# Mixer B of an encoder layer: the per-token factor reaches all partitions through DRAM instead of through TensorE

## The chip, the core and the metric

The kernel runs on one core of one Trainium2 chip. The time is the device time of one execution in microseconds (us), the median of three runs. Profiles are of one execution each. PE is TensorE's matmul, PEld its weight load, DVE is VectorE, ACT ScalarE, POOL GpSimd; SP is the engine that issues all DMAs here.

## The reference, cut to what matters

One encoder layer is applied to two batches that share weights: "p" with 512 tokens and "s" with 1024. A normalised input is projected to 9728 columns, cut into the queries, keys, values and gates of three mixers and three merge gates. The three mixers' outputs, each times SiLU of its gate path, are projected, merged, projected again and added to the input. The change is in mixer B, differential attention:

```
a = jax.nn.softmax(s - slopes * dist, axis=-1)
w = a[:, :, 0] - lam * a[:, :, 1]
o = jnp.einsum('bhqk,bkhe->bqhe', w, v)
o = rms_norm(o, g_diff) * (1.0 - lam_init)
...
pb = (yb * jax.nn.silu(zb)) @ w_br_b
```

So each token and head has one number, its RMS factor together with the softmax denominator, that multiplies the 128 values of that token and head.

## The kernel before

**A program that is ordered by a planner.** The code records operations on tiles; `Program.order` then plays them through a list schedule with assumed prices (`price`, `shared`) and fixes one order for each engine, and `emit` (line 486, so every row of the profile carries L486) writes the instructions out in that order. An operation is placed when its operands are ready in the plan, its engine is free, a buffer slot of its class is free (`SLOTS`, `CAPS`), and it lies within `AHEAD` operations of the oldest one not placed. `copy` and `tt` record several ways (ACT or DVE, DVE or POOL), of which the planner picks one. On the chip every engine works through its own list strictly in order, SP too: a DMA whose operand is not ready holds all DMAs behind it.

**The stages.** First the projection of batch p (tiles `raw`, split into high and low parts `wh`, `wl`, `wb`, multiplied with `tp`/`th`/`tl` into PSUM tiles `p`, added up in `c`, stored to `Up`, `Us`, `Vp`, `Vs` in DRAM). From some 440 us on, the mixers of p, and then those of s, are interleaved with the projection of batch s: both give PE, DVE and ACT work at the same time. After some 1500 us come the branch projections and merge gates (`merge`) and the output projection (`output`).

**Mixer B** (`mixer_b`) has four units, one for each head, for each batch. A unit fetches its gate `z_tile` into `y`, makes scores `s`, exponentials `e` (or `tab`), transposes the weights (`t` to `pt`, `pl`) and multiplies with V into `o`, four blocks of 128 tokens into one PSUM bank `o`, with the value channels on partitions and 512 tokens along the free axis. After each 512 tokens it closes: squares of `o` are summed over the channels by four one-column matmuls with `ones`, so the sums stand with tokens on partitions, in a [128, 4] tile `r`, part of `czb`. DVE, POOL (a power of -1/2) and DVE make the factor there. It is needed along the free axis on all 128 partitions. Before the change, four `pe.transpose` of a broadcast column of `r` against `ident` put it into a PSUM tile `t`, and DVE multiplies `y` (gate times `o` times the gain `gd`) by that. `y` then goes to `YG` in DRAM, and is read again only in the merge stage. This closing runs 12 times: 4 units with one block of 512 tokens in p, 4 with two in s.

Mixer C (`mixer_c`) has the same need and already goes through DRAM: a transposed factor is written to `FD`, and read back with a partition step of zero into tiles `bb`. `bb` has two tiles of 2 KB per partition, of the class `k2` of 18 slots, which `ws`, `wh`, `wl`, `c`, `y`, `ft`, `pt` and others share.

Of the kernel before, what the change touches and what calls it, by code (L numbers as in the profile page):

```python
# [8 lines left out]
F32 = mybir.dt.float32  # L9
# [3 lines left out]
OP = mybir.AluOpType  # L13
# [50 lines left out]
def rows(a, off, dims):  # L64
    return bass.AP(tensor=a.tensor, offset=a.offset + off, ap=[list(d) for d in dims])
# [464 lines left out]
def build(ctx, tc, a):  # L530
    nc = tc.nc
    pg = Program(tc, nc, SLOTS, CAPS)
    act, dve, pool, pe = pg.act, pg.dve, pg.pool, pg.pe

    dma = pg.sync.dma_start

    def static(shape, name):
        return pg.tile("static", shape, F32, name)

    def load(dst, src, off, dims):  # L540
        dma(dst, src.rows(off, dims) if isinstance(src, View) else rows(src, off, dims))
# [18 lines left out]
    def tt(dst, x, y, op, engines="DP"):  # L560
        pg.any(*[({"D": dve, "P": pool}[e], "tensor_tensor", (dst, x, y), {"op": op}) for e in engines])

    def split(hi, lo, x, scale=None, psum=False):

        copy(hi, x, scale)
        if scale is None:
            tt(lo, x, hi.bitcast(F32), OP.subtract, "D" if psum else "DP")
        else:
            dve.scalar_tensor_tensor(lo, x, scale, hi.bitcast(F32), op0=OP.mult, op1=OP.subtract)

    ident = static([128, 128], "ident")
# [416 lines left out]
    def fetch(s, col, L):  # L988

        if L == 512:  # L990
            t = pg.tile("stp", [128, 512], F32)
            dma(t, U[s][col // 128][0])
        else:
            t = pg.tile("stg", [128, 1024], F32)
            dma(t.rearrange("p (b t) -> p b t", b=2), U[s][col // 128].rearrange("b p t -> p b t"))
        return t
# [29 lines left out]
    def q_tiles(x, L, view, scale=None):  # L1026
        q = qk_tiles(2, L)
        for f, g in pieces(x, view, L):
            for j in range(2):
                s, d = 64 * j, 64 - 64 * j  # L1030
                split(g(q[j], s, s + 64), g(q[j], d, d + 64), f(x, s, s + 64), scale)
        return q

    def k_tiles(x, L, view):
        kh, kl = qk_tiles(2, L), qk_tiles(2, L)
        for j in range(2):
            s, d = 64 * j, 64 - 64 * j
            pool.memset(kl[j][d:d + 64].bitcast(F32), 0.0)
            for f, g in pieces(x, view, L):
                split(g(kh[j], s, s + 64), g(kl[j], s, s + 64), f(x, s, s + 64))  # L1040
                copy(g(kh[j], d, d + 64), f(x, s, s + 64))
        return kh, kl
# [15 lines left out]
    def z_tile(s, col, b):  # L1058

        y = pg.tile("y", [128, 512], F32)  # L1060
        dma(y, U[s][col // 128][b])
        t = pg.tile("ft", [128, 512], F32)
        act.activation(t, y, AF.Tanh, scale=0.5)
        dve.scalar_tensor_tensor(y, t, 1.0, y, op0=OP.add, op1=OP.mult)
        return y

    def e_tile():
        return pg.tile("e", [128, 1024], F32)
# [99 lines left out]
    def mixer_b(sq, u, L):  # L1168
        nh = L // 512
        c0 = 128 * u  # L1170
        if sq not in dist:
            dist[sq] = pg.tile("tab", [128, 2304], F32)[:, :1920]
            dma(dist[sq], a["c_dist"])
        q = q_tiles(fetch(sq, QB + c0, L), L, nat, 0.125 / SLOPE_B[u])
        kh, kl = k_tiles(fetch(sq, KB + c0, L), L, nat)
        v = pg.tile("vp" if nh == 1 else "v", [128, 2, 4 * nh, 128], F32R)
        v = [v[:, 0], v[:, 1]]
        vr = pg.tile("stp" if nh == 1 else "stg", [128, 4 * nh, 128], F32)
        load(vr, V[sq][VB + 256 * (u // 2)], 128 * (u % 2), [[256, 128], [128 * 256, 4 * nh], [1, 128]])
        split(v[0], v[1], vr)  # L1180
        ww = []
        yield
        for i in range(L // 128):
            if nh == 1:
                pair = e_tile()
                pair = [pair[:, :512], pair[:, 512:]]
            elif i % 2:
                pair = pg.tile("tab", [128, 2, 1024], F32)
                pair = [pair[:, 0], pair[:, 1]]
            else:  # L1190
                pair = [e_tile(), e_tile()]
            if i % 4 == 0:
                y = z_tile(sq, ZB + c0, i // 4)
            st = small(6, "stb")
            es = []
            for hf in range(nh):
                pss = [pg.tile("s", [128, 512], F32) for _ in range(2)]
                qk_scores(pss, q, kh, kl, lambda t: t[:, 128 * i:128 * i + 128],
                          lambda t: t[:, 512 * hf:512 * hf + 512])
                x0 = 512 * hf - 128 * i + 896  # L1200
                for m in range(2):
                    dve.tensor_tensor_reduce(
                        out=pair[m][:, 512 * hf:512 * hf + 512], in0=pss[m], in1=dist[sq][:, x0:x0 + 512],
                        scale=-SLOPE_B[u], scalar=3e38 if hf == 0 else st[:, m:m + 1],
                        op0=OP.add, op1=OP.min, accum_out=st[:, 2 * hf + m:2 * hf + m + 1])
            for m in range(2):
                e = pair[m]
                nm = st[:, m:m + 1] if nh == 1 else st[:, 2 + m:3 + m]
                act.activation(e[:, :L], e[:, :L], AF.Exp, scale=-1.0, bias=nm, accum_out=st[:, 4 + m:5 + m])
                es.append(e)  # L1210
            if i % 4 == 0:
                cz = small(12, "czb")
            z0, c1 = cz[:, i % 4:i % 4 + 1], cz[:, 4:5]
            dve.reciprocal(z0, st[:, 4:5])
            dve.reciprocal(c1, st[:, 5:6])
            dve.scalar_tensor_tensor(c1, st[:, 4:5], c1, neglam, op0=OP.mult, op1=OP.mult)
            w = es[0][:, :L]
            dve.scalar_tensor_tensor(w, es[1][:, :L], c1, w, op0=OP.mult, op1=OP.add)
            ww.append(w)
            if i % 2 == 0:  # L1220
                yield
                continue
            if i % 4 == 1:
                o = pg.tile("o", [128, 512], F32)
            oq = o[:, 256 * (i // 2 % 2):256 * (i // 2 % 2) + 256]
            for b in range(2 * nh):
                ps = pg.tile("t", [128, 2, 256], F32)
                for k in range(2):
                    for j in range(2):
                        c = 256 * b + 128 * k  # L1230
                        pe.transpose(ps[:, k, 128 * j:128 * j + 128], ww[j][:, c:c + 128], ident)
                ph = pg.tile("pt", [128, 2, 256], F32R)
                pl = pg.tile("pl", [128, 2, 256], F32R)
                split(ph, pl, ps, psum=True)
                for k in range(2):
                    kb = 2 * b + k
                    for n, (x, z) in enumerate(((v[0], ph), (v[1], ph), (v[0], pl))):
                        pe.matmul(oq, x[:, kb], z[:, k], start=kb + n == 0, stop=kb == 4 * nh - 1 and n == 2)
            ww = []
            if i % 4 == 1:  # L1240
                yield
                continue
            sq_ = pg.tile("ft", [128, 512], F32)
            act.activation(sq_, o, AF.Square)
            ps = pg.tile("t", [128, 512], F32)
            for j in range(4):
                pe.matmul(ps[:, j:j + 1], sq_[:, 128 * j:128 * j + 128], ones, start=True, stop=True)
            r = cz[:, 8:12]
            dve.scalar_tensor_tensor(r, ps[:, :4], 1.0 / 128, cz[:, :4], op0=OP.mult, op1=OP.mult)
            dve.scalar_tensor_tensor(r, r, 1.0, cz[:, :4], op0=OP.mult, op1=OP.mult)  # L1250
            pool.tensor_scalar(r, r, EPS, None, op0=OP.add)
            pool.tensor_tensor(r, r, mhalf, op=OP.pow)
            dve.tensor_tensor(r, r, cz[:, :4], op=OP.mult)
            ps = pg.tile("t", [128, 512], F32)
            for j in range(4):
                pe.transpose(ps[:, 128 * j:128 * j + 128], r[:, j:j + 1].to_broadcast([128, 128]), ident)
            dve.scalar_tensor_tensor(y, o, gd, y, op0=OP.mult, op1=OP.mult)
            dve.tensor_tensor(y, ps, y, op=OP.mult)
            store_yg(sq, i // 4, 4 + u, y)
            yield  # L1260

# [392 lines left out]
    j = done = slot = 0  # L1654
    for i, k in slots("s", TS):
        slot = i + k / 7
        while j < len(units) and slot > starts[j]:
# [7 lines left out]
            j, done = j + 1, 0  # L1665
# [44 lines left out]
```

## Time and profile before

| what | value |
| --- | --- |
| median of three runs | 1846.41 us (1845.9 to 1847.65) |
| the profiled execution | 1845.54 us |
| its span, first to last instruction | 1843.8 us |
| PE / DVE / ACT / POOL busy | 98% / 84% / 66% / 18% of the span |
| mean granted TensorE clock | 0.996 |

The profiled execution took 1.74 us more than its span, and 0.87 us less than the median. In the rows below, a busy share is of the span or of the window that the row names; a row of groups gives the total busy time, the mean of one, and how long the engine stood idle right before such an instruction.

### The profile page before, as it was taken

The page shows a single profiled execution, that of the slowest core. Times are in us where ns is not written, and L with a number is a line of the kernel's source. Part 1 is how long each engine was busy: PE and PEld are TensorE (multiplying, and loading weights), DVE is VectorE, ACT ScalarE, POOL GpSimd, SP SyncE. Part 2 cuts the span into 40 slices and gives each one's busy share as a digit, 9 for nine tenths or more (in the row PEclk, how much of TensorE's full clock was granted, in tenths as well). Part 3 has the DMA queues.
Part 4 walks back from the last instruction along what each step waited for, and adds up shares of the span by engine and source line. Part 5 has one row for each costly group of instructions (what it writes and reads, how often), then busy time and mean ns, then how long its engine had stood idle before and what let it go on. Part 6 is the DMA issues. An engine that isn't in the chain of part 4 may idle for free.

```text
span 1843.8 us, 32386 instructions
## 1 busy us (share of the span) xinstructions
PE 1802.0 (98%) x11353; PEld 1466.4 (80%) x11448; DVE 1546.3 (84%) x3081; ACT 1209.4 (66%) x2411; POOL 328.1 (18%) x284
## 2 busy tenths in 40 slices
PE   7999999999999999999999999999999999999998
PEld 6999999999988777778787877776777776666776
DVE  8879999997887678788989898868779887876886
ACT  7677878894556766665656565777678786643343
POOL 0000000000000000000000000000001144987874
PEclk9999999999999999999999999999999999999999
DMA  7645545453424455642323231445455557977641
GB/s 245 184 145 178 172 149 193 152 182 115 140 90 142 135 151 158 183 149 92 103 84 127 65 120 69 132 125 168 133 150 158 179 162 257 325 235 252 213 150 69
DMA packets 242336, 287.14 MB, mean 156 GB/s; under 512 B 33182, under 2 KB 168574, under 8 KB 242174
## 3 DMA queue, kind: packets, MB, share of 16 engines
q1 hardware_dynamic: 242174, 285.08, 48.6%
q8 instruction: 90, 1.47, 0.3%
q14 instruction: 72, 0.59, 0.1%
HBM read 203.93 MB, written 81.44 MB: 155 GB/s over the span
## 4 chain that ended last, share of the span: by engine, by line
PE 93%; DVE 3%; ACT 2%; issue 1%; DMA 0%; SPq 0%; POOL 0%; DVEq 0%; POOLq 0%; ACTq 0%
PE p L486 64%; PE s L486 16%; PE o L486 6%; PE t L486 6%; ACT qk L486 1%; DVE qk L486 1%; DVE e L486 0%; ACT c L486 0%; DMA xp<-x_prompt 0%; DVE wl L486 0%; DVE c L486 0%; DVE tab L486 0%; DVE ws L486 0%; DVE xt L486 0%; ACT tab L486 0%
## 5 line engine op out<-in xcount | busy, mean ns | idle before, releaser
L486 PE MATMUL p<-th,wh 128*128 128x512 f32 x1400 | 428.5, 414 | 0.1
L486 PEld LDWEIGHTS p<-th,wh 128*128 128x128 f32 x1400 | 252.9, 189 | 53.7 <-issue 5.8
L486 PE MATMUL p<-th,wl 128*128 128x512 f32 x1016 | 295.2, 400 | 0.2 <-DVE wl L486 0.2
L486 ACT ACTIVATE wb<-raw 128x512 bf16<-128x512 f32 (+1 forms) x254 | 155.0, 614 | 145.0 <-PE p L486 89.8
L486 ACT ACTIVATE c<-p 128x512 f32<-128x512 f32 (+1 forms) x291 | 144.8, 498 | 125.4 <-PE p L486 122.3
L486 PEld LDWEIGHTS p<-th,wl 128*128 128x128 f32 x1016 | 186.3, 188 | 39.1 <-issue 2.9
L486 PEld LDWEIGHTS <-wb 128*128 128x128 bf16 x1392 | 109.1, 98 | 105.2 <-issue 50.2
L486 PE MATMUL s<-qk 128*128 128x512 f32 (+5 forms) x736 | 186.9, 361 | 4.7 <-DVE qk L486 2.2
L486 DVE TENSOR_TENSOR wl<-ws,wh 128x512 fp32r<-128x512 f32 x251 | 179.1, 716 | 11.8 <-ACT wh L486 6.5
L486 DVE CUSTOM_DVE_ANT_0 e<-s,tab 128x384 f32<-128x384 f32 (+3 forms) x256 | 130.3, 533 | 51.0 <-PE s L486 48.6
L486 DVE TENSOR_TENSOR c<-p,c 128x512 f32<-128x512 f32 (+1 forms) x219 | 125.2, 577 | 50.6 <-PE p L486 36.7
L486 ACT ACTIVATE pt<-t 128x512 fp32r<-128x512 f32 (+3 forms) x193 | 100.7, 539 | 101.3 <-PE t L486 99.1
L486 DVE TENSOR_TENSOR wl<-raw,wh 128x512 fp32r<-128x512 f32 x212 | 155.6, 746 | 6.1 <-ACT wh L486 2.6
L486 ACT ACTIVATE wh<-ws 128x512 fp32r<-128x512 f32 x240 | 147.7, 621 | 13.4 <-DVE ws L486 10.6
L486 ACT ACTIVATE wh<-raw 128x512 fp32r<-128x512 f32 (+1 forms) x228 | 136.7, 606 | 22.5 <-PE s L486 11.1
L486 PE MATMUL p<-tl,wb 128*128 128x512 bf16 x527 | 145.2, 381 | 5.3 <-issue 0.8
L486 PE MATMUL p<-tp,wh 128*128 128x256 f32 x888 | 147.2, 294 | 2.4 <-ACT wh L486 2.4
L486 PEld LDWEIGHTS s<-qk 128*128 128x128 f32 (+1 forms) x736 | 124.5, 189 | 29.3 <-issue 4.6
L486 PE MATMUL p<-tp,wl 128*128 128x256 f32 x888 | 142.7, 283 | 0.0
L486 ACT ACTIVATE e<-e,st 128x384 f32<-128x384 f32 (+2 forms) x192 | 105.2, 550 | 36.3 <-DVE st L486 35.4
L486 POOL MEMSET qk<- 64x512 f32 (+1 forms) x48 | 35.8, 747 | 515.8 <-PE t L486 171.1
L486 PE MATMUL p<-wq,th 128*128 128x256 f32 x816 | 124.6, 292 | 0.0
(231 smaller groups left out, 3752.7 us busy)
## 6 DMA issues: line engine op xcount, KB each, us to landing
raw<-w_in SPq DMA_DIRECT2D x140, 512.0 KB
Us<-c SPq DMA_DIRECT2D x128, 256.0 KB
Up<-c SPq DMA_DIRECT2D x64, 256.0 KB
stg<-Us SPq DMA_DIRECT2D x30, 512.0 KB
g<-Us SPq DMA_DIRECT2D x48, 256.0 KB
tab<-E SPq DMA_DIRECT2D x192, 48.0 KB
stp<-Up SPq DMA_DIRECT2D x30, 256.0 KB
YG<-y SPq DMA_DIRECT2D x30, 256.0 KB
```

The costliest lines, as they stand in the source:

```text
L486: getattr(engs[o.eng], o.meth)(*[val(x) for x in o.args], **{k: val(x) for k, x in o.kw.items()})
```

## The change

The four transposes and their PSUM tile go. The factor `r` ([128 tokens, 4 blocks]) is written to a DRAM tensor `RB` as four rows of 128 floats, which is 512 single floats side by side for the DMA, since neighbours in DRAM lie on different partitions. It is read back into a `bb` tile with a partition step of zero: 128 partitions get the same 512 floats. The multiplication of `y` takes `bb` in place of PSUM's `t`, and through `tt` the planner may give it to DVE or POOL.

```diff
--- before.py
+++ after.py
@@ -1251,11 +1251,12 @@
             pool.tensor_scalar(r, r, EPS, None, op0=OP.add)
             pool.tensor_tensor(r, r, mhalf, op=OP.pow)
             dve.tensor_tensor(r, r, cz[:, :4], op=OP.mult)
-            ps = pg.tile("t", [128, 512], F32)
-            for j in range(4):
-                pe.transpose(ps[:, 128 * j:128 * j + 128], r[:, j:j + 1].to_broadcast([128, 128]), ident)
+            RB = pg.tile("dram", [4, 128], F32, "RB")
+            dma(RB.rows(0, [[1, 128], [128, 4]]), r)
+            rb = pg.tile("bb", [128, 512], F32)
+            load(rb, RB, 0, [[0, 128], [1, 512]])
             dve.scalar_tensor_tensor(y, o, gd, y, op0=OP.mult, op1=OP.mult)
-            dve.tensor_tensor(y, ps, y, op=OP.mult)
+            tt(y, rb, y, OP.mult)
             store_yg(sq, i // 4, 4 + u, y)
             yield
```

The planner makes a new order, from the first closing on. All 12 multiplications stay on DVE. PE's order differs from row 2207 of 6238 to row 4467, which is from about 480 to some 1220 us; ahead of and behind that it is the same, and so are ACT's and DVE's; SP's order too is the same again from its row 446 of 744.

**PE, the first closing of batch p** (`czb` is the factor's tile, `wq`, `th` are projection operands, `ones`, `ft` the sums of squares):

```order
 L486 MATMUL s<-qk 128x512 x4
-L486 MATMUL p<-wq,th 128x256 x25
-L486 MATMUL t<-ident,czb 128x128 x4
-L486 MATMUL p<-wq,th 128x256 x23
+L486 MATMUL p<-wq,th 128x256 x48
 L486 MATMUL s<-qk 128x512 x4
 L486 MATMUL t<-ident,e 128x128 x2
```

The four transposes stood between 25 and 23 projection matmuls of one product; now the 48 stand in one piece.

**SP, the last closing of batch s in mixer B, before** (`v` is the V tile and `stg` a staging tile of the units that follow, `Us` a projection's result):

```order
L486 DMA v<-Vs_508 64x4x128 x2
L486 DMA YG_341<-y 128x512
L486 DMA stg<-Us_465 128x2x512
L486 DMA stg<-Us_453 128x2x512
L486 DMA Us_476<-c 128x512
```

and the same place in the changed kernel:

```order
L486 DMA v<-Vs_508 64x4x128 x2
L486 DMA RB<-czb 128x4x1
L486 DMA stg<-Us_465 128x2x512
L486 DMA bb<-RB 128x512
L486 DMA stg<-Us_453 128x2x512
L486 DMA YG_341<-y 128x512
L486 DMA Us_476<-c 128x512
```

The write and the read of `RB` are new in SP's list, a `stg` load stands between them, and the store of `y` has moved behind both `stg` loads.

**DVE, the same closing in the changed kernel**, from right behind the last step of the factor (`czb<-czb`) to its use:

```order
L486 CAST wh<-raw 128x512
L486 TENSOR_TENSOR wl<-raw,wh 128x512
L486 ISA e,st_15123<-s,tab 128x384
L486 ISA st_15123 128x1
L486 ISA e,st_15123<-s,tab 128x384
L486 ISA st_15123 128x1
L486 COPY pt<-t 128x384
L486 CAST wh<-ws 128x512
L486 TENSOR_TENSOR ws<-ws,raw 128x512
L486 TENSOR_TENSOR wl<-ws,wh 128x512
L486 TENSOR_TENSOR ws<-raw 128x512
L486 TENSOR_TENSOR y<-bb,y 128x512
```

The multiplication, the last row, has moved down: nine larger instructions now stand between the factor and its use.

## Rows read from the trace of the kernel before

**Rows 1.** the page's part 1: engine, busy us, share of the span, instructions

```profile
PE 1802.0 (98%) x11353; PEld 1466.4 (80%) x11448; DVE 1546.3 (84%) x3081; ACT 1209.4 (66%) x2411; POOL 328.1 (18%) x284
```

**Rows 2.** the page's part 4: shares of the chain that ended last, by engine

```profile
PE 93%; DVE 3%; ACT 2%; issue 1%; DMA 0%; SPq 0%; POOL 0%; DVEq 0%; POOLq 0%; ACTq 0%
```

**Rows 3.** busy time by stage: window, length, five engines, PEclk, DMA share, GB/s

```profile
480.00:1160.00 680.00, 675.91 (x3863) 538.15 (x3906) 578.93 (x1300) 425.90 (x813) 34.59 (x50) 1.00 0.38 119
...
1170.00:1180.00 10.00, 5.87 (x24) 3.59 (x22) 9.14 (x11) 9.93 (x12) 0.95 (x1) 0.85 0.59 228
1180.00:1190.00 10.00, 10.00 (x54) 8.78 (x53) 8.05 (x16) 5.74 (x8) 0.00 (x0) 0.81 0.42 131
...
1500.00:1843.80 343.80, 330.42 (x1534) 231.44 (x1560) 264.47 (x360) 170.37 (x354) 251.03 (x189) 0.99 0.64 213
```

**Rows 4.** groups by shape, PE: busy us, mean ns, idle before

```profile
L486 PE MATMUL t<-ident,czb 128*128 128x128 f32 x48 | 7.2, 272 | 0.0
```

**Rows 5.** chain of waits, two spots: start us, us, what

```profile
484.49 0.44 PE t L486 x4
...
1141.90 0.44 PE t L486 x4
```

**Rows 6.** groups by shape, DVE

```profile
L486 DVE TENSOR_TENSOR wl<-ws,wh 128x512 fp32r<-128x512 f32 x251 | 179.1, 716 | 11.8 <-ACT wh L486 6.5 <-PE p L486 3.4 <-issue 0.4
...
L486 DVE TENSOR_TENSOR ws<-raw 128x512 f32<-128x512 f32 x138 | 94.1, 684 | 3.8 <-PE o L486 3.4 <-PE p L486 0.4
...
L486 DVE CUSTOM_DVE_ANT_0 e<-s,tab 128x384 f32<-128x384 f32 x96 | 50.9, 553 | 22.9 <-PE s L486 21.7 <-PE t L486 0.4
...
L486 DVE CAST wh<-ws 128x512 fp32r<-128x512 f32 x32 | 17.5, 548 | 1.1 <-PE o L486 1.1
...
L486 DVE TENSOR_TENSOR y<-t,y 128x512 f32<-128x512 f32 x12 | 8.3, 691 | 3.9 <-PE t L486 3.8
...
L486 DVE TENSOR_TENSOR y<-bb,y 128x512 f32<-128x512 f32 x6 | 4.2, 692 | 0.2
```

**Rows 7.** timeline of SP's DMA issues: start us, us

```profile
635.75 0.34 SPq L486 DMA_DIRECT2D FD<-pt  x1
636.18 0.37 SPq L486 DMA_DIRECT2D stp<-Up  x1
637.15 2.48 SPq L486 DMA_DIRECT2D bb<-FD  x4
```

**Rows 8.** instructions on bb and FD: ns min/median/max, first and last start

```profile
L486 DVE TENSOR_TENSOR bb<-bb,qk x12: 681/685/687, 644.0 to 1376.2; 128x512 f32<-128x512 f32 x12
L486 SPq DMA_DIRECT2D FD<-pt x4: 317/342/367, 635.8 to 1361.6; - x4
```

**Rows 9.** SP's waits, whole span: us in total, times, longest

```profile
SPq L486 <- DVE c L486: 373.7, 98, 21.6
...
SPq L486 <- DMA S<-st: 3.5, 1, 3.5
```

**Rows 10.** SP's waits, 1150 to 1200 us

```profile
SPq L486 <- DVE wl L486: 11.1, 1, 11.1
```

**Rows 11.** all engines' waits, 440 to 1400 us

```profile
ACT qk L486 <- DMA stg<-Us: 1.0, 1, 1.0
```

**Rows 12.** chain of waits, 1155 to 1185 us

```profile
1157.70 0.71 PE o L486 x6
...
1174.30 1.98 ACT qk L486
...
1176.30 1.93 ACT qk L486
...
1178.93 1.22 PE p L486 x2
...
1182.71 1.28 PE o L486 x6
```


## The prediction

> **What bounds the kernel now.** I read the page's shares first, then the chain that ended last, then the busy time by stage, and last the stretch that the change touches. PE is busy 98% of the span, DVE 84%, ACT 66% [rows 1]; the chain is 93% PE, and no DMA or DMA queue has even 1% of it [rows 2]. By stage this holds where the mixers run: from 480 to 1160 us PE is busy 675.91 of 680 us, DVE 578.93, ACT 425.90 [rows 3]. PE idles 4.1 us there in all, so a microsecond less of PE work is a microsecond less of time, unless an engine that feeds PE comes too late. The largest hole lies right behind: of 1170 to 1180 us PE is busy 5.87, an idle 4.1 us, and the granted clock is 0.85 in this window and 0.81 in the next [rows 3]. The last part, behind 1500 us, has 13.4 us of PE idle [rows 3], but its instructions keep their order, so I leave it as it is.
>
> **What is removed.** 48 transposes of 128x128 [rows 4]. Three readings of their price are at hand. The mean of one is 272 ns, which would be 13.1 us for 48; but matmuls overlap in PE's pipeline. The group's busy time is 7.2 us [rows 4], in which the pipeline's tail at each group of four, that other matmuls overlap, is still counted. The chain gives what one group of four pushes away: 0.44 us, at the closing at 484 us as at the one at 1142 us [rows 5], 0.11 us for one. I take the chain, since it counts no time twice: 12 x 0.44 = 5.3 us. PE never stood idle before these transposes [rows 4], so they filled no hole that would stay open without them.
>
> For this price the Trainium skill has another figure (TensorE: Matmul & The Clock Gate, Part 4: PE-mode transpose): about 275 ns for one 128x128 transpose among other work, most of it access latency. The 272 ns of [rows 4] agree as a duration of one; used as a price it would make the gain 13 us, against 5.3 by the chain, where the next transpose starts 0.11 us later. It is a rival below.
>
> DVE's multiplication costs the same from PSUM as from `bb`: 691 against 692 ns [rows 6], so nothing. It had waited 3.8 us in 8 cases for the transposes [rows 6]; DVE does not set the pace, so this counts as nothing too. A PSUM bank of the two for `t` comes free a little earlier: nothing, or a small gain inside the range.
>
> **What is added.** 24 DMA issues. The nearest rows are those of `FD` in mixer C, 342 ns for the write, and 2.48 us for four reads of `bb`, 0.62 us each with the gaps [rows 7, 8]: 12 x (0.34 + 0.62) = 11.5 us of SP's time. SP covers it: it waits for `c` alone 373.7 us [rows 9]. Its own bound is zero below, and above what stands behind it: loads of `raw` and `stg` that come later. From 440 to 1400 us the longest that ACT waits for a transfer is 1.0 us [rows 11], so by this row the loads come ahead of their use. I take zero.
>
> The path of the factor gets longer. The write of `FD` is issued at 635.75 and its read at 637.15 [rows 7], so a write is known to have landed 1.4 us after its issue starts; this holds for long pieces, and the nearest row for small ones is a wait of 3.5 us for `S` [rows 9], with 16-byte pieces. The read takes at least its issue of 0.6 us, and at most the 4.4 us from the end of the four issues (639.63) to the first use of `bb` at 644.0 [rows 7, 8], which DVE may have made late for other reasons. So the round trip is 2.0 us (1.4 + 0.6) to 8.5 us (3.5 + 0.6 + 4.4); I take 5, the middle. What hides it: `y` is wanted only in the merge stage hundreds of microseconds later, so only the multiplication itself can wait, with DVE's list behind it. At the last closing the order has nine instructions between factor and multiplication, which by the rows of their kinds take 548 + 716 + 553 + 553 + 553 + 548 + 684 + 716 + 684 ns = 5.6 us (the copy of 384 columns taken like the score instruction of 384) [rows 6]. A trip of 5 us is covered even here; of 8.5 us, 2.9 us would be seen. Ten of the twelve closings have some 20 rows in that place, so they have more cover. At three of the twelve the read stands right behind the write in SP's list, so SP stands still for the landing, 1.4 to 3.5 us, and what is queued behind it (two `raw` loads and a `YG` store) leaves that much later: 4.2 to 10.5 us of SP's waits in all, hidden as above. `y` and the `bb` slot are held some 5 to 10 us longer; a `k2` slot fewer can hold back a `ws` or `wh` of the next product. No row prices that; from below it is nothing, and from above what one late feed has cost, the hole below.
>
> On small transfers the Trainium skill speaks against the change (DMA: Bandwidth & Descriptors, the section on the two cost components): every DMA pays about 2.0 us, most of it until the last byte is known to be written. Two in a row would make the trip 4.0 us; the 1.4 us of [rows 7] is shorter for a write. With 4.0 the sum stays as it is, the 5.6 us cover both.
>
> **What is moved.** From the first closing to the last all three compute engines get new neighbours. The place where that can count is the hole at 1170 us. In the chain PE waits there for ACT: two strided splits `qk<-stg` of 1.98 and 1.93 us one behind the other, until 1178.24, and then runs at the lower clock: six `o` matmuls take 1.28 us where they took 0.71 before [rows 12]. So from 1178.93 to 1183.99 (1182.71 + 1.28) it works at 0.71/1.28 = 0.55 of its speed, a loss of 2.3 us. The hole costs 4.1 + 2.3 = 6.4 us. In the new order ACT has the same five splits and the same two exponentials at this place; only the first split stands later and one of the last two earlier. I take it as unchanged, with bounds of -6.4 us (gone) and about twice itself.
>
> **Sum.** 1845.54 us for the profiled execution less 5.3 is 1840.2 us; the median of the runs stands 0.87 us above that execution, so 1841.1 us is forecast, -0.29%. A measurement of this kernel can tell some 0.2% (3.7 us) from no change.
>
> **Rivals.**
> - *Feeders take PE's place.* The 5.3 us become PE idle, because the next PSUM result or weight split comes when it came before. For it: DVE is busy 85% in the stretch, and the hole at 1170 us shows PE waiting for ACT. Against it: 4.1 us of idle in 680 us. Time: 1846.4 us.
> - *The read is held in SP's list, and DVE with it: slower.* At the last closing a `stg` load stands between the write and the read. A load waits until its slot is free; in this neighbourhood SP stood 11.1 us for a DVE instruction [rows 10]. If it stands so long between write and read, the multiplication comes 11.1 + 5 us after the factor, DVE has 5.6 us of other work, and stands 10.5 us; PE runs dry after it and loses 2.3 us more by the clock. Against it: in the list before, the two `stg` loads stood at this same place behind the store of `y`, and a slot that is free then is not waited for. Time with one such case: 1841.1 + 12.8 = 1853.9 us. It decides (over 0.2% slower) from a loss of 5.3 + 3.7 = 9.0 us.
> - *The hole at 1170 us closes* by the new neighbours: 1841.1 - 6.4 = 1834.7 us. For it: the ACT list there is a little different. Against it: the five splits still must run, and PE needs them.
> - *Transposes at their full duration:* 1846.41 - 13.1 = 1833.3 us. Against it stand the 0.44 us of the chain.
>
> **How the numbers follow.** Forecast 0.53; of this 0.07 lies above 1842.7 us, within 0.2% of before, since small losses at twelve places add up to a microsecond or two. Feeders 0.22, held read 0.14, closed hole 0.08, full duration 0.03. Faster: 0.46 + 0.08 + 0.03 = 0.57; same: 0.22 + 0.07 = 0.29; slower: 0.14. The forecast's own range is 1838.5 to 1844 us. For 8 in 10 the range takes in the feeders and half of the closed hole below, and of the slower case those with a small loss: 1835 to 1848.5 us.
>
> **What would show it.** Right: no `t<-ident,czb` on PE, its busy time about 5 to 7 us lower, all of it between 480 and 1200 us; `y<-bb,y` 18 times at 692 ns with almost no idle before; SP with 24 issues on `RB`. The feeders' case shows as PE idle between 480 and 1160 us grown from 4 to some 9 us. The held read shows as DVE idle before `y<-bb,y` for a DMA, and SP's wait ahead of it. The hole at 1170 to 1190 us with its clock says at once whether it closed or grew; a second such hole elsewhere would make the forecast wrong, and the row of that window would name it.

## The result, and the profile after

The changed kernel takes 1897.88 us (median of four runs, 1896.99 to 1899.3) against 1846.16 us before (1844.63 to 1847.65): a ratio of 1.0284, with a 95% interval of 1.0272 to 1.0296. It is 51.7 us slower. 1841.1 us was forecast, and the top of the range was 1848.5 us.

The page's first part, the answer to [rows 1] (busy us, share of the span, instructions of each engine):

```profile
span 1895.2 us, 32320 instructions
PE 1813.7 (96%) x11306; PEld 1472.8 (78%) x11400; DVE 1539.9 (81%) x3069; ACT 1216.5 (64%) x2423; POOL 328.5 (17%) x284
```

and the view of the cores, with the mean granted clock:

```profile
core 0: 1895.2 us, clock 0.986
```

The span grew by 51.4 us. PE's idle time (span less busy) grew from 41.8 to 81.5 us, that is by 39.7; PE's busy time grew by 11.7 us although 7.2 us of transposes [rows 4] are gone. Busy time grew since matmuls ran slower: a granted clock of 0.986 over 1895.2 us is 26.5 us below full speed, one of 0.996 over the span before was 7.4 us, 19.1 us less. So the loss is idle time of PE, and half as much again for the clock. (Both profiles lack some 95 matmul records, 11353 of 11448 and 11306 of 11400 by the weight loads, so each idle figure is somewhat high; what counts is how much it grew.)

The windows tell where, the answer to [rows 3] (start and end; length; busy us of PE, PEld, DVE, ACT and POOL, each with its instructions; granted clock, DMA share, GB/s):

```profile
0.00:480.00 480.00, 466.79 (x3901) 448.88 (x3901) 426.73 (x789) 357.29 (x716) 13.98 (x23) 1.00 0.53 171
480.00:1160.00 680.00, 641.50 (x3580) 508.37 (x3620) 532.80 (x1199) 406.75 (x777) 34.90 (x48) 0.97 0.41 119
480.00:490.00 10.00, 10.00 (x78) 9.50 (x79) 9.02 (x24) 7.62 (x16) 1.56 (x2) 1.00 0.13 23
490.00:500.00 10.00, 7.01 (x57) 6.27 (x55) 2.81 (x7) 4.54 (x9) 1.21 (x2) 1.00 0.53 139
500.00:510.00 10.00, 8.52 (x55) 7.71 (x56) 8.19 (x18) 3.63 (x9) 0.00 (x0) 0.83 0.34 111
1220.00:1230.00 10.00, 5.68 (x26) 3.66 (x25) 9.74 (x11) 9.90 (x12) 0.95 (x1) 0.93 0.44 165
```

Ahead of 480 us PE is as busy as before. From 480 to 1160 us PE was idle 4.1 us before and now 38.5 us (680 less 641.50). The three small windows are the first closing: DVE is busy 2.81 of 10 us, PE idles 3 us, and in the next window the granted clock is 0.83, so that part of it ran at the lower level of 1.2 GHz. The last row is the old hole of 1170 us, which has moved back with everything else; PE is busy 5.68 us there, against 5.87 before.

The chain of waits through that first closing (start, length in us, what), which answers to [rows 5], names the cause:

```profile
483.35 0.08 DVE czb L486
483.43 0.02 issue
483.44 9.81 DMA RB<-czb
493.25 0.02 issue
493.27 6.84 DMA bb<-RB
500.11 0.02 issue
500.13 0.04 DVE y L486
...
500.74 0.69 DVE pl L486
501.43 0.04 issue
501.48 1.57 PE o L486 x6
```

The write of 2 KB in 512 pieces of 4 bytes takes 9.81 us until SP can issue the read, and the read takes another 6.84 us. Then come the multiplication, DVE's next instruction `pl`, and six `o` matmuls on PE that waited for `pl`. They take 1.57 us; at full clock six took 0.71 us [rows 12].

The events of three closings in the timeline (start, length, engine, operation, tiles; in brackets the engine's idle time before it and who ended that), as for `FD` in [rows 7, 8]: the first, the one with the fastest landing, and the last.

```profile
483.44 0.36 SPq L486 DMA_DIRECT2D RB<-czb  x1
493.27 0.33 SPq L486 DMA_DIRECT2D bb<-RB  x1
500.13 0.69 DVE L486 TENSOR_TENSOR y<-bb,y 128x512 f32<-128x512 f32 x1 [5.27 <-DMA bb<-RB]
...
922.15 0.37 SPq L486 DMA_DIRECT2D RB<-czb  x1
931.13 0.32 SPq L486 DMA_DIRECT2D bb<-RB  x1
936.13 0.69 DVE L486 TENSOR_TENSOR y<-bb,y 128x512 f32<-128x512 f32 x1 [4.50 <-DMA bb<-RB]
...
1243.27 0.55 SPq L486 DMA_DIRECT2D RB<-czb  x1
1254.85 0.33 SPq L486 DMA_DIRECT2D bb<-RB  x1
1259.01 0.69 DVE L486 TENSOR_TENSOR y<-bb,y 128x512 f32<-128x512 f32 x1 [5.80 <-DMA bb<-RB]
```

From the write's issue to the read's issue, called the landing below, it is 9.0 us (922.15 to 931.13) in the shortest of the twelve closings and 12.6 us in the longest; from the read's issue to the multiplication another 3.4 to 6.9 us. A landing can be too long, since other issues of SP may stand between the two, so the shortest of a kernel says most. The round trip is 14.0 to 17.0 us, 15.4 in the mean. At the last closing DVE was ready for the multiplication 9.9 us after the write's issue (15.74 less 5.80), and stood 5.8 us.

The sums over the kernel, as waits (total us, times, longest), of DVE, of SP and of PE; the first answers to DVE's wait for the transposes in [rows 6], the second to SP's in [rows 9]:

```profile
DVE y L486 <- DMA bb<-RB: 52.5, 11, 5.8
...
SPq L486 <- DMA RB<-czb: 84.5, 12, 10.3
...
PE o L486 <- DVE pl L486: 22.3, 8, 4.5
...
PE t L486 <- DVE tab L486: 9.5, 3, 4.1
```

DVE, which works in order, stands at 11 of 12 multiplications, 4.8 us each; PE waits for DVE's `pl` 22.3 us, where it was 0.4 us before, and for its `tab` 9.5 us instead of 1.9.

### The profile page after: what moved, and what is told of

Same layout as the page of the kernel before. It is cut to its first block, busy times and chain, and to the rows that moved or that the text cites. A ratio compares the mean times of both kernels' runs of the same rounds, so it can differ in the third digit from the quotient of the medians.

```text
span 1895.2 us, 32320 instructions
## 1 busy us (share of the span) xinstructions
PE 1813.7 (96%) x11306; PEld 1472.8 (78%) x11400; DVE 1539.9 (81%) x3069; ACT 1216.5 (64%) x2423; POOL 328.5 (17%) x284
## 4 chain that ended last, share of the span: by engine, by line
PE 84%; DMA 6%; DVE 5%; ACT 3%; issue 2%; SPq 0%; POOL 0%; DVEq 0%; POOLq 0%; ACTq 0%
PE p L486 58%; PE s L486 15%; PE o L486 6%; PE t L486 5%; DMA RB<-czb 3%; DMA bb<-RB 2%; ACT qk L486 1%; DVE qk L486 1%; DVE e L486 1%; DMA stp<-Up 1%; DVE y L486 1%; ACT c L486 0%; DVE wl L486 0%; DVE ws L486 0%; SPq L486 0%
## 5 line engine op out<-in xcount | busy, mean ns | idle before, releaser
L486 PEld LDWEIGHTS p<-th,wl 128*128 128x128 f32 x1016 | 187.5, 190 | 39.7 <-issue 2.6
L486 PEld LDWEIGHTS <-wb 128*128 128x128 bf16 x1392 | 108.9, 98 | 106.3 <-issue 51.4
L486 ACT ACTIVATE pt<-t 128x512 fp32r<-128x512 f32 (+4 forms) x189 | 98.7, 540 | 114.4 <-PE t L486 112.6
L486 PE MATMUL t<-ident,e 128*128 128x128 f32 x672 | 120.8, 276 | 11.0 <-DVE e L486 7.0
```

The lines of the kernel that those rows point to most:

```text
L486: getattr(engs[o.eng], o.meth)(*[val(x) for x in o.args], **{k: val(x) for k, x in o.kw.items()})
```

## The experiments

The theories: A, DVE's stand at the multiplication is the loss. B, SP's stand behind the write is, since it holds back the other transfers. C, the small pieces disturb other transfers. On why the write is slow: P, it has many pieces (512); Q, every write and read by way of DRAM has such a price; S, pieces of 4 bytes are slow (S1: a price for each piece, S2: a fixed one); N, only 4-byte pieces that land side by side are. Times are medians, ratios are to the kernel before on the same chip (1845.5 to 1845.7 us) with their 95% interval. In the edits, `...` marks what is left out.

**e1_nofactor** has neither transposes nor transfers: the removal alone.

```diff
-            RB = ...; dma(RB.rows(...), r); rb = ...; load(rb, RB, ...)
-            tt(y, rb, y, OP.mult)
+            tt(y, y, y, OP.mult)
```

> Leaves out the factor: no transposes, no RB, and the last multiplication is y by y (SBUF, 692 ns as before). It shows what the removal of 48 transposes and a new order are worth by themselves. If the loss of 51.7 us comes from the round trip through DRAM (waits), the time is 1846.2 - 5.3 = 1840.9 us, within 1838 to 1845. If the new order of the planner is to blame, this kernel, which gets a new order from the same place on, stays well above 1850 us.

1842.67 us, 0.9984 [0.9975, 0.9994]: a gain of 2.9 us (1.1 to 4.6), somewhat below the 5.3 of the chain. The loss is not in what was removed, nor in there being a new order from the first closing on; this kernel's order is its own, though, not that of the change.

**e2_late** has the same instructions as the change, but the planner is told that the write lands 5.5 us later than it thought and the read 2.5 us later, so that it puts other work ahead.

```diff
             dma(RB.rows(0, [[1, 128], [128, 4]]), r)
+            slow(5.5)
             load(rb, RB, 0, [[0, 128], [1, 512]])
+            slow(2.5)
```

> The changed kernel, with the planner told that the write of RB lands 5.5 us later and the read 2.5 us later than it assumed; instructions and bytes are the same. Theory A (DVE stands before y<-bb because that was placed 9 us behind the factor and the trip takes 15 us): DVE's 52.5 us of waits fall under 10 us and the time comes to 1841 to 1850 us. Theory B (SP's 84.5 us of standing for RB hold other transfers): the read moves down in SP's list too, so SP's wait for RB falls as well, and the time also recovers; the runs of the next call separate the two. Theory C (6144 pieces of 4 bytes disturb the other transfers): nothing recovers, about 1895 us.

1849.06 us, 1.0019 [1.001, 1.0029]. The landing is as slow as in the change, as one closing in the timeline shows:

```profile
860.92 0.37 SPq L486 DMA_DIRECT2D RB<-czb  x1
871.60 0.32 SPq L486 DMA_DIRECT2D bb<-RB  x1
878.23 0.68 DVE L486 TENSOR_TENSOR y<-bb,y 128x512 f32<-128x512 f32 x1
```

The write takes 10.7 us, the multiplication comes 17.3 us after the write's issue, and DVE doesn't stand there (no bracket). The waits of the whole kernel:

```profile
DVE y L486 <- DMA bb<-RB: 1.4, 2, 0.9
SPq L486 <- DMA RB<-czb: 44.7, 8, 10.6
```

With DVE's wait at 1.4 us, 48.8 of the 51.7 us are back. C falls as the main cause: the small pieces are all there, and the loss is not. SP's stand fell to 44.7 us as well, so B is not yet out.

**e6_defer** parts them: the read stays right behind the write in SP's list, only the multiplication moves down.

```diff
+            slow(0.0)
             load(rb, RB, 0, [[0, 128], [1, 512]])
+            slow(10.0)
```

> The changed kernel, with the planner told that the read of bb lands 10 us later than assumed, and nothing told about the write: the read stays two to five places behind the write in SP's list, so SP stands for the landing as in the changed kernel, while y<-bb moves down in DVE's list. Theory A: SP's waits for RB stay near 84 us in all, DVE's for bb fall under 10 us, and the time is 1843 to 1853 us. Theory B: about 1885 to 1900 us.

1850.21 us, 1.0024 [1.0014, 1.0034]; DVE never waits for `bb`, and SP stands as long as in the change (its wait, total us, times, longest):

```profile
SPq L486 <- DMA RB<-czb: 84.8, 12, 9.5
```

So SP's full stand of 84.8 us goes with a loss of 4.5 us against before, not of 52: A holds, B as the main cause falls.

**e7_pool** is the opposite: POOL issues both transfers, so that SP never stands, and DVE still waits.

```diff
-            dma(RB.rows(0, [[1, 128], [128, 4]]), r)
+            pool.dma_start(RB.rows(0, [[1, 128], [128, 4]]), r)
-            load(rb, RB, 0, [[0, 128], [1, 512]])
+            pool.dma_start(rb, RB.rows(0, [[0, 128], [1, 512]]))
```

> The changed kernel with both transfers issued by POOL in place of SP, so SP never stands for RB, while y<-bb stays some nine to ten us behind the factor in DVE's list. Theory A: DVE still waits some 4 us or more at each closing, and the time stays above 1880 us, more if POOL's issue is slower than SP's. Theory B: the time falls to 1843 to 1855 us.

1881.79 us, 1.0196 [1.0179, 1.0212], with DVE's wait at 46.0 us in 12 cases:

```profile
DVE y L486 <- DMA bb<-RB: 46.0, 12, 5.3
```

Without SP's stand 36 us of the loss remain: A again. The 16 us less than in the change come with 6.5 us less of DVE's wait and a free SP; how they divide is not shown.

**e5_side** is the kernel before, with the write and a read that nobody uses: C and SP's stand, without DVE's.

```diff
                 pe.transpose(ps[:, 128 * j:128 * j + 128], r[:, j:j + 1].to_broadcast([128, 128]), ident)
+            RB = pg.tile("dram", [4, 128], F32, "RB")
+            dma(RB.rows(0, [[1, 128], [128, 4]]), r)
+            rb = pg.tile("bb", [128, 512], F32)
+            load(rb, RB, 0, [[0, 128], [1, 512]])
```

> The kernel before with its four transposes, and beside them the write of 512 pieces of 4 bytes to RB and the read to bb, which no instruction uses: no engine but SP can wait for the trip. Theory A (DVE's wait at y<-bb is the loss): 1845 to 1850 us. Theory B (SP's standing for the landing, some 7 us at 12 places, holds other transfers and with them PE) or C (the small pieces disturb other transfers): most of the 51 us is there, 1875 to 1900 us.

1853.54 us, 1.0044 [1.0029, 1.0059]: 7.9 us for both transfers, SP's stand (75.4 us) and the order that goes with them. That is 3.5 us above what A gave and far below what B or C gave, so neither is the main cause. ACT waits up to 3.9 us for late loads of `stp`, `raw` and `stg` here. The trip also holds others than SP: for `wh` and `wl` ACT and DVE wait 3.7 us in all on the read of `bb`, which shares their slots. How the 7.9 us divide between SP's stand, these slots and the order stays open.

**e3_16B** asks for the write's shape: `RB` lies as [128, 4], so that each partition writes its four factors in one piece of 16 bytes, and the multiplication reads `bb` in that order.

```diff
-            RB = pg.tile("dram", [4, 128], F32, "RB")
-            dma(RB.rows(0, [[1, 128], [128, 4]]), r)
+            RB = pg.tile("dram", [128, 4], F32, "RB")
+            dma(RB, r)
...
-            tt(y, rb, y, OP.mult)
+            y4 = y.rearrange("c (j p) -> c j p", j=4)
+            tt(y4, rb.rearrange("c (p j) -> c j p", j=4), y4, OP.mult)
```

> The write in 128 pieces of 16 bytes (RB is [token in block][block], the multiplication reads bb in a permuted order) in place of 512 pieces of 4 bytes. Theory P (the landing goes with the number of pieces, 9.8 us for 512): the write lands in about 2.5 to 4 us after its issue, the trip is 6 to 10 us, DVE waits under 2 us for each closing, and the time is 1842 to 1860 us. Theory Q (a write to DRAM followed by its read has a fixed price of some 10 us): SP still waits some 8 us each and the time stays at 1880 to 1900 us.

1841.5 us, 0.998 [0.997, 0.9989]: the whole computation, and faster than both kernels. One of the shortest landings in the timeline:

```profile
856.96 0.32 SPq L486 DMA_DIRECT2D RB<-czb  x1
858.50 0.32 SPq L486 DMA_DIRECT2D bb<-RB  x1
```

The same 2 KB land within 1.54 us (1.52 in the shortest of the twelve), and SP's wait falls from 84.5 to 14.6 us in 9 cases; DVE never waits for `bb`, though with its strided operand the multiplication takes 1.07 us (median of all 18 `y<-bb,y`, 12 of them strided) in place of 0.69.

**e4_512B** goes further: one transpose of `r` on PE and a copy, and four pieces of 512 bytes.

```diff
+            ...
+            pe.transpose(ps[:4, :128], r, ident)
+            ...
+            dve.tensor_copy(fr[:4, :128], ps[:4, :128])
             RB = pg.tile("dram", [4, 128], F32, "RB")
-            dma(RB.rows(0, [[1, 128], [128, 4]]), r)
+            dma(RB, fr[:4, :128])
```

> One transpose of r ([128, 4] to [4, 128]) on PE, a copy on DVE, then a write of 4 pieces of 512 bytes, as mixer C does for FD. Theory P: the write lands about 1.4 to 2.5 us after its issue, DVE's waits for bb fall under 2 us for each closing, PE does 12 transposes (1.3 us) in place of 48: 1843 to 1856 us. Theory Q: as for the 16-byte pieces, 1880 to 1900 us.

1843.35 us, 0.9989 [0.9979, 0.9998]; the shortest landing is 1.21 us:

```profile
996.58 0.27 SPq L486 DMA_DIRECT2D RB<-pt  x1
997.79 0.33 SPq L486 DMA_DIRECT2D bb<-RB  x1
```

Q is out: by way of DRAM the exchange need not be slow. Size or number of the pieces is left.

**e8_512x16** keeps 512 pieces but makes each 16 bytes (every factor four times).

```diff
+            ...
+            dve.tensor_copy(r4..., r....to_broadcast([128, 4, 4]))
-            dma(RB.rows(0, [[1, 128], [128, 4]]), r)
+            dma(RB.rows(0, [[4, 128], [512, 4], [1, 4]]), r4.rearrange("p (j c) -> p j c", c=4))
```

> The changed kernel, where each factor is written four times side by side, so the write has 512 pieces of 16 bytes in place of 512 of 4 (one small DVE copy more at each closing); the read still takes 512 floats, so the factors it multiplies by are not the right ones. Theory P (the landing goes with the number of pieces): the write lands some 9 to 12 us after its issue as in the changed kernel, and the time stays near 1895 us. Theory S (pieces of 4 bytes are what is slow, 16 bytes are not): 1.5 to 4 us, as with 128 pieces of 16 bytes, and the time falls to 1842 to 1850 us.

1839.26 us, 0.9967 [0.9952, 0.9983], a little below what S gave; the shortest landing is 2.45 us:

```profile
899.78 0.37 SPq L486 DMA_DIRECT2D RB<-rx  x1
902.23 0.32 SPq L486 DMA_DIRECT2D bb<-RB  x1
```

P is out.

**e9_128x4** writes 128 pieces of 4 bytes, the first of the four columns, and reads these 512 bytes four times into each partition.

```diff
...
-            dma(RB.rows(0, [[1, 128], [128, 4]]), r)
+            dma(RB.rows(0, [[1, 128], [128, 1]]), r[:, 0:1])
...
-            load(rb, RB, 0, [[0, 128], [1, 512]])
+            load(rb.rearrange("p (j c) -> p j c", j=4), RB, 0, [[0, 128], [0, 4], [1, 128]])
```

> The changed kernel, writing only the first of the four columns of factors: 128 pieces of 4 bytes in place of 512 (the other three blocks are multiplied by the factors of the first, and the read takes each row four times, in 512 pieces of 512 bytes). Theory S1 (each piece of 4 bytes costs some 15 ns, (9.0 - 1.2) us / 512): the shortest gap from the write's issue to the read's falls from 9.0 to some 3 us. Theory S2 (a write of 4-byte pieces has a fixed price): the gap stays near 9 us.

1957.02 us (two runs), 1.0604 [1.0583, 1.0625], the slowest of all. The closing with the shortest landing in the timeline:

```profile
890.44 0.32 SPq L486 DMA_DIRECT2D RB<-czb  x1
897.56 0.37 SPq L486 DMA_DIRECT2D bb<-RB  x1
907.83 0.69 DVE L486 TENSOR_TENSOR y<-bb,y 128x512 f32<-128x512 f32 x1 [10.22 <-DMA bb<-RB]
```

and DVE's wait in all:

```profile
DVE y L486 <- DMA bb<-RB: 111.1, 12, 10.8
```

A quarter of the pieces still takes 7.1 us at least, where S1 gave 3 and S2 9: each piece has no fixed price of its own, and S1 falls. The read, 512 pieces from the same 512 bytes, takes 8.6 to 10.9 us until DVE can use it, where the change's 128 pieces of 2 KB took 3.4 to 6.9. DVE's wait doubled, and the loss too: 111.4 us against 51.7, for 111.1 against 52.5 us of wait. That is A once more, from the other side.

**e10_apart** writes the 512 pieces of 4 bytes 64 bytes apart (into a tensor filled ahead) and reads its first 512 floats.

```diff
+    RBS = pg.tile("dram", [512, 16], F32, "RB")
+    ...
-            dma(RB.rows(0, [[1, 128], [128, 4]]), r)
+            dma(RBS.rows(0, [[16, 128], [2048, 4]]), r)
...
```

> The changed kernel with its 512 pieces of 4 bytes written 64 bytes apart (the read takes the first 512 floats of that area, most of them ones, so the factors are not the right ones). Theory N (it is slow because neighbouring floats of one stretch of DRAM come from different pieces, so writes to the same line follow one another): the shortest gap from the write's issue to the read's falls to 2 to 4 us and the time to some 1842 to 1850 us. Theory S (a piece of 4 bytes is slow wherever it goes): the gap stays at 9 to 12 us and the time near 1895 us.

1840.92 us, 0.9977 [0.9966, 0.9987], a little below what N gave. The shortest landing in the timeline:

```profile
900.55 0.37 SPq L486 DMA_DIRECT2D RB<-czb  x1
902.43 0.32 SPq L486 DMA_DIRECT2D bb<-RB  x1
```

The same number of pieces of the same size in a closely similar order (some 190 of DVE's 3071 instructions stand elsewhere), and the landing takes 1.88 us instead of at least 9.0; SP's wait is 9.6 us in 5 cases. S falls, and N is right in that 4-byte pieces are slow only side by side. Its reason, that writes to the same line follow one another, was not tested. One thing more differs here: the tensor had been filled ahead, and all twelve closings use the same one.

**e12_512x8** writes 512 neighbouring pieces of 8 bytes.

```diff
...
-            dma(RB.rows(0, [[1, 128], [128, 4]]), r)
+            dma(RB.rows(0, [[2, 128], [256, 4], [1, 2]]), r4.rearrange("p (j c) -> p j c", c=2))
```

> As the version with 512 pieces of 16 bytes, with 512 pieces of 8 bytes (each factor twice; the factors are not the right ones). If the landing goes with the bytes below 16, the shortest gap lies between 2.5 and 9 us; if only 4-byte pieces are slow, it is about 2.5 us and the time 1839 to 1843 us; if all below 16 bytes are alike, 9 us and near 1895 us.

1840.29 us, 0.9969 [0.9958, 0.998]; the shortest landing is 3.2 us:

```profile
593.11 0.37 SPq L486 DMA_DIRECT2D RB<-rx  x1
596.32 0.32 SPq L486 DMA_DIRECT2D bb<-RB  x1
```

That is the first of the three cases, near its lower end. Twice the length takes two thirds of the time away, so neighbourhood alone is not slow: 4-byte pieces side by side are.

**e11_pool_mul** is e3_16B with the strided multiplication on POOL.

```diff
-            tt(y4, rb.rearrange("c (p j) -> c j p", j=4), y4, OP.mult)
+            pool.tensor_tensor(y4, rb.rearrange("c (p j) -> c j p", j=4), y4, op=OP.mult)
```

> The version with 128 pieces of 16 bytes, its 12 multiplications given to POOL in place of DVE. DVE loses 12 x 1.07 = 12.8 us of work, and a late read can no longer hold DVE. If DVE's work beside PE counts at all, 1837 to 1841 us; if not, as the 16-byte version, 1841.5 us; if POOL on the port it shares with DVE slows DVE, 1843 to 1848 us.

1841.37 us, 0.9978 [0.9969, 0.9988]: the same as e3_16B. But DVE's busy time did not fall with it, 1545.5 us against 1546.1: the planner gave DVE some 3 us of other work, and DVE's other instructions took some 10 us longer in all (`ws<-ws,raw` 716 ns in the mean, 695 in e3_16B). That is what the expectation's third case supposed, POOL slowing DVE, though not the time that it gave, and no run isolates it. So this run doesn't tell whether DVE's work beside PE counts; it shows only that POOL can take the multiplication without a loss.

## Why the prediction was wrong, step by step

**The step that failed** is the length of the factor's path: "So the round trip is 2.0 us (1.4 + 0.6) to 8.5 us (3.5 + 0.6 + 4.4); I take 5, the middle." It is 14.0 to 17.0 us. The greater part of the error is the write: 1.4 to 3.5 us were taken from the rows of `FD` (16 pieces of 512 bytes [rows 7]) and `S` (16-byte pieces [rows 9]), and 9.0 to 12.6 us came out. Neither row has neighbouring pieces of 4 bytes, which the change's access pattern showed; it was the thing not in the trace, and the bound above was drawn from rows that differ from it in just what counts. e3_16B, e4_512B and e10_apart show that for other shapes the bound was sound (1.2 to 1.9 us in their shortest landings). The read's 0.6 to 4.4 us were nearer: 3.4 to 6.9.

**What hung on it.** "A trip of 5 us is covered even here" would have held for 8.5 us too: at the last closing DVE came to the multiplication 9.9 us after the write's issue, not 5.6. Against 15.4 us no cover of this order is enough, and not the last closing alone stands but 11 of 12. The "some 20 rows" at the other closings covered no more: where DVE stood, it had come to the multiplication 8.7 to 12.5 us after the write's issue (the trip less the wait of each).

**Size of the loss.** Between e10_apart and the change the write's addresses are the difference that was meant, beside some change of order: 1.0284 less 0.9977 is 3.1%, 57 us. e6_defer, with DVE's wait gone and SP's stand kept, has 48 us less than the change; the 9 us between it and e10_apart go with SP's stand and the moved order, and were not divided. For 52.5 us of DVE's wait PE idled 39.7 us more and lost 19 us by the clock.

**SP's stand** was taken as zero, with three closings of 1.4 to 3.5 us. It was twelve and 84.5 us, since the few loads between write and read are issued long before a landing of 9 us. By e6_defer and e5_side this is worth a few us, up to 9: a second, smaller miss with the same root.

**What came out right.** The removal was set at 5.3 us by the chain: e1_nofactor gives 2.9 (1.1 to 4.6), and the kernels with a quick landing and no transposes are 4.0 (e3_16B) to 6.4 us (e8_512x16) faster than before, none near the 13.1 of the full duration. Each of these kernels has an order of its own, so the price of the transposes alone is not isolated, and 5.3 lies above e1_nofactor's interval. The multiplication takes 692 ns as before. The two issues of a closing take 0.37 and 0.32 us, less together than the 0.34 and 0.62 reckoned. The hole of 1170 us stayed.

**The rivals.** The held read had the right last link, DVE before `y<-bb,y` with PE dry behind it and the clock down, but for another reason (a slot of `stg`) and at one closing only; one such case was priced at 12.8 us, and the eleven cost about 5 us each (57/11). The hole did not close. What feeders would have kept of the 5.3 us can't be seen beside 39.7 us of new idle time.

On the small writes the Trainium skill (DMA: Bandwidth & Descriptors, Specifications) gives 512 bytes as the least transfer for line rate, and says that below it the DMA engine does a read-modify-write. No run shows that step. For the landing the runs agree only in part: 16 bytes (1.5 us) land about as fast as 512 (1.2 us), and it is at 4 bytes, and only side by side, that most time is lost. The 2.0 us that the same page of the Trainium skill gives for a DMA's fixed part (quoted ahead) stand above these two landings and far below the change's 9.0.

## What to carry to other kernels

Before pricing a transfer from another row of the trace, compare not the bytes but the shape at the far end: piece length, and whether pieces of a few bytes land side by side. Here one permuted layout (each partition's four floats in one piece of 16 bytes, and a strided operand at the use) made a loss of 52 us into a gain of 4. And where an engine works its list in order, a transfer that lands later than the list was planned for can cost about the whole wait, as here (52.5 us of DVE's wait, 51.7 us of loss): if the transfer can't be quickened, tell the planner the measured time, as in e2_late.

## What the runs showed of the hardware

Shortest times from the issue of the write to the issue of a read that waits for it, all of data written to DRAM and each from one profile:

| pieces | where | us |
|---|---|---|
| 4 x 512 B | side by side | 1.2 |
| 128 x 16 B | side by side | 1.5 |
| 512 x 4 B | 64 B apart | 1.9 |
| 512 x 16 B | side by side | 2.45 |
| 512 x 8 B | side by side | 3.2 |
| 128 x 4 B | side by side | 7.1 |
| 512 x 4 B | side by side | 9.0 |

Neighbouring pieces of 4 bytes are far out of line with the rest, and a quarter of them takes not a quarter of the time. The traces' records of single DMA packets say where that time is not. In the change's closing at 922 us all 512 pieces of 4 bytes, and the 16 more records of 4 bytes that come with them, begin and end within 1.28 us of the write's issue, and so they do in e10_apart's closing at 901 us; yet SP can issue the read only after 9.0 us in the one and after 1.9 us in the other. So by these records it is not the DMA engines' handling of the pieces that takes long, but what follows until the write is known to have landed. Why side by side this takes so long is not shown by any run. Reads of the same bytes have a price too: 128 pieces from the same 2 KB took 3.4 to 6.9 us until use, 512 pieces from the same 512 bytes 8.6 to 10.9 us; whether the number of pieces or the narrow source does it was not parted. A wait of 5.3 us of DVE was enough, in the first closing, for 3 us of PE idle in the window from 490 us, and a granted clock of 0.83 in the window behind.
